# Layer 0's whole expert blocks in three products of rounded parts, with every third low part on GpSimd and a weight ring of ten

## The chip, the cores and the metric

The kernel runs on one core of a Trainium2 chip. A core has a matrix engine (TensorE, PE in the rows; PEld is its weight load), VectorE (DVE), ScalarE (ACT), GpSimd (POOL) and a queue that issues DMAs (SyncE, SP). The metric is the device time of one execution in microseconds, as the median of several runs. One execution is profiled; every row below is from that one.

## The reference, cut to what matters

Two layers. Each runs attention over 256 context and 256 latent tokens, then a mixture of experts. Layer 0 sends all 512 tokens through its experts, layer 1 only the 256 latent ones.

```
def swiglu(h, wg, wu, wd):
    return (jax.nn.silu(h @ wg) * (h @ wu)) @ wd

def moe(h, w_router, b_router, wg, wu, wd, sg, su, sd):
    ...                                  # gate: two of 16 experts for each token
    y = swiglu(h, sg, su, sd)            # the shared expert
    for e in range(N_EXPERTS):
        y = y + gate[..., e:e + 1] * swiglu(h, wg[e], wu[e], wd[e])
    return y
```

All arrays are float32. An expert's gate and up matrices are 1024 x 512, its down matrix is 512 x 1024: 2 MB each.

## The kernel before, in words

**Blocks and groups.** The chosen token slots of layer 0's experts are packed into 11 blocks of 128 rows. The most loaded of 14 experts has 128 slots, the next six have 96, the other seven 64, and two fixed experts have 128 each. So blocks 0, 9 and 10 hold one expert each ("whole" blocks), the others two, or parts of two with quarters of 32 rows. `GROUPS` orders them: [7, 8], [0, 6], [4, 5], [1, 2, 3], [9, 10]. A group runs all its gate products (`first`, then `silu`), all its up products (`first`, then `middle`), and its down products (`second`). Within a group each expert's matrix is loaded once (`matrix`, `got`). While a group's down products run, the next group's rows, gathered by indirect DMA (`bring`, `fetch`), are turned by TensorE (`turned`).

**Products.** Before, all expert blocks of layer 0 multiply plain float32 (`columns`): a block with several experts issues narrow products side by side, 64 or 32 columns wide, a whole block one of 128 columns. A plain float32 product shows in the trace as two instructions. Other matrices, the shared expert among them, are multiplied in rounded parts: `Stream.pieces` takes a loaded 128 x 2048 buffer in two pieces of 1024, ACT copies it to a high part of type float32r, DVE subtracts to get the low part, and `mm3` makes three products (high by high, high by low, low by high).

**Buffers.** Expert weights come through a ring of 1 MB buffers (`Stream.buf`): four of `rawp` and six of `raw2`, ten in all. The part buffers of the shared expert (`wpool`, three high and three low) are given back after group 2 (`w_es.close()`), and three more raw buffers take their place (`stE.further`, `RAW4`). `stE` is the stream of the loads, `stD` that of the part buffers. `shared_second`, the shared expert's down product, comes behind group 1.

**The end of the stage.** Blocks 0 to 8 scatter their results to DRAM (`scatter`). These are read back (`row_back`) in the last group into buffers of `raw2` and summed by `add_rows`: for each of four row tiles three operations on POOL for columns 0 to 511 and the same three on DVE for 512 to 1023. Blocks 9 and 10 keep their results on the chip as parts (`kept`). Behind a branch (`tc.If`, line 1643, for slots beyond the blocks) they are spread to the tokens' rows by products with a 0/1 matrix, `hits` (line 1687), which `own_rows` makes with eight comparisons. Layer 1 starts from there.

**Order.** A planner orders each engine's instructions when the program is built, from the program's order and a model of their times. On the chip each engine runs its own queue in order. Nothing is moved across the branch.

Of the kernel before, what the change touches and what calls it, by code (L numbers as in the profile page):

```python
# [11 lines left out]
F32 = mybir.dt.float32  # L12
F32R = mybir.dt.float32r
# [6 lines left out]
P = 128  # L20
D = 1024
KC = D // P
# [24 lines left out]
RAW4 = 3  # L47
# [12 lines left out]
SECOND_AT = 1  # L60
# [2 lines left out]
HIA = (5, 5)  # L63
RAW2 = 6
FPARTS = 3
EVERY = 5
GQ_AT = 10
STAT = 3
RAW3 = (4, 10)
# [69 lines left out]
def build(tc, I, out, dbg=None):  # L139
# [3 lines left out]
    def pool(st, name, bufs=1, **kw):  # L143
        if kw.get("space") is None:
            kw["reuse_waits"] = "tile"
        return st.enter_context(tc.tile_pool(name=name, bufs=bufs, **kw))
# [21 lines left out]
    def sc_bank(name="sc"):  # L168
        return pq.tile([P, 512], F32, tag="mm", name=name)

    def tr_bank(name="tr"):
        return pt.tile([P, 512], F32, tag="tr", name=name)

    def f(ap):
        return ap.bitcast(F32)
# [222 lines left out]
    def load_gq(l):  # L398
        nc.gpsimd.dma_start(out=gq, in_=I["gq"][l:l + 1].to_broadcast([P, 2 * QK + 2 * HD]))

    def layer(l):
# [341 lines left out]
        def evac(i, o, src):  # L743
            (nc.scalar.copy if i % 2 == 0 else nc.vector.tensor_copy)(out=o, in_=src)
# [461 lines left out]
        def shares(b):  # L1206

            qs_ = QUARTERS[l][4 * b:4 * b + 4]
            n = 4 if qs_[0] == qs_[3] else 2 if qs_[0] == qs_[1] and qs_[2] == qs_[3] else 1
            return [(32 * i, 32 * n, qs_[i]) for i in range(0, 4, n)]  # L1210

        def columns(o, x, ws, start, stop):

            for c0, n, w in ws:
                js_ = slice(c0, c0 + n)
                nc.tensor.matmul(o[js_], x[:, js_], w, start=start, stop=stop, tile_position=(0, c0))  # L1216
# [198 lines left out]
        else:  # L1415
# [50 lines left out]
            yprev = []  # L1466
            stE = Stream(tc, [rawp] + raw2)

            def shared_second():
                for blk in range(2):  # L1470
                    pbs = [mm_bank() for t in range(NT)]
                    for i, ws in enumerate(stD.pieces(stE.raw(I["w_s_down"][l, blk], 4, 512), 4, 512)):
                        for t in range(NT):
                            th, tl = (ep.tile([P, 2, P], F32R, tag="s" + c, name="s" + c, bufs=2) for c in "hl")
                            split(th, tl, sh[:, 2 * i:2 * i + 2, t * P:(t + 1) * P])
                            for k in range(2):
                                mm3(pbs[t], th[:, k], tl[:, k], *ws[k], i == 0 and k == 0, i == 1 and k == 1)
                    for t in range(NT):
                        add_result(t, blk, pbs[t], ep.tile([P, 512], F32, tag="hs", name="tm"))
# [9 lines left out]
            def evac(i, o, src):  # L1489
                return (nc.scalar.copy if i % 2 == 0 else nc.vector.tensor_copy)(out=o, in_=src)  # L1490

            eb = [3]

            def turned(x_):

                xt = ep.tile([P, KC, P], F32, tag="xt", name="xt", bufs=eb[0])
                for half_ in range(2):
                    tb = tr_bank()
                    for k in range(4):
                        kk = half_ * 4 + k  # L1500
                        nc.tensor.transpose(tb[:, k * P:(k + 1) * P], x_[:, kk * P:(kk + 1) * P], ident)
                    evac(half_, xt[:, half_ * 4:half_ * 4 + 4], tb.rearrange("p (k s) -> p k s", k=4))
                return xt

            def first(xt, ws):

                pb = sc_bank("pgu")
                for k in range(KC):
                    columns(pb, xt[:, k], [(c0, n, w[k // 4][:, k % 4]) for c0, n, w in ws], k == 0, k == KC - 1)
                return pb  # L1510

            def silu(pg):
                h_ = ep.tile([P, 512], F32, tag="hs", name="hs")
                ACT(h_, pg, AF.Silu)
                return h_

            def middle(h_, pu, gate_):

                tb = pm.tile([P, 512], F32, tag="md", name="ht")
                ht = ep.tile([P, 4, P], F32, tag="ht", name="ht", bufs=eb[0])  # L1520
                nc.vector.scalar_tensor_tensor(out=h_, in0=pu, scalar=gate_, in1=h_, op0=ALU.mult, op1=ALU.mult)  # L1521
                for k in range(4):
                    nc.tensor.transpose(tb[:, k * P:(k + 1) * P], h_[:, k * P:(k + 1) * P], ident)
                evac(1, ht, tb.rearrange("p (k s) -> p k s", k=4))
                return ht

            def second(ht, ws, yo, rest=None):
                for b in range(2):
                    pb = m2_bank()
                    for k in range(4):  # L1530
                        columns(pb, ht[:, k], [(c0, n, w[b][:, k]) for c0, n, w in ws], k == 0, k == 3)
                    x = slice(b * 512, (b + 1) * 512)
                    if rest is None:
                        evac(b, yo[:, x], pb)
                    else:
                        split(yo[:, x], rest[:, x], pb)
# [12 lines left out]
            def matrix(nm, got, b):  # L1549

                ws = []
                for c0, n, r in shares(b):
                    if r not in got:
                        got[r] = [stE.raw(s_, 4, 512) for s_ in halves(nm, by_rank(r))]
                    ws.append((c0, n, got[r]))
                return ws
# [8 lines left out]
            def own_rows():  # L1565

                h_ = ep.tile([P, 2 * NT, P], F32R, tag="xt", name="hits", bufs=eb[0])
                rowf = ep.tile([P, 2 * NT], F32, tag="rowf", name="rowf", bufs=1)
                for i, b in enumerate(own):
                    for t in range(NT):  # L1570
                        x = i * NT + t
                        TS(out=rowf[:, x:x + 1], in0=tab[:, b, 0:1], scalar1=float(-t * P), scalar2=None, op0=ALU.add)
                        TS(out=h_[:, x], in0=iota_r, scalar1=rowf[:, x:x + 1], scalar2=None, op0=ALU.is_equal)
                return h_
            X = [turned(x_) for x_ in bring(GROUPS[l][0])]
            for g_, g in enumerate(GROUPS[l]):
                nxt = GROUPS[l][g_ + 1] if g_ + 1 < len(GROUPS[l]) else []
                xg = bring(nxt)
                if g is own:
                    hits = own_rows()  # L1580
                got = {}
                hg = [silu(first(x_, matrix("w_e_gate", got, b))) for x_, b in zip(X, g)]
                got = {}
                H = [middle(h_, first(x_, matrix("w_e_up", got, b)), f(tab)[:, b, 1:2]) for h_, x_, b in zip(hg, X, g)]
                got = {}
                X = []
                for i, b in enumerate(g):
                    w = matrix("w_e_down", got, b)
                    if b == own[0]:
                        k_ = fp_.tile([P, 2, D], F32R, tag="sh", name="kept", bufs=1)  # L1590
                        kept[b] = k_[:, 0], k_[:, 1]
                    if b == own[1]:
                        kept[b] = yo_tile(F32R), yo_tile(F32R)
                    if b in own:
                        second(H[i], w, *kept[b])
                    else:
                        yo = yo_tile()
                        second(H[i], w, yo)
                        scatter(yo, tab[:, b, 2:3])
                    X += [turned(x_) for x_ in (xg[i:] if i + 1 == len(g) else xg[i:i + 1])]  # L1600
                if g_ == 0:
                    for s in strs:
                        get_row(gt2[:, s], l, 3, s)
                if g_ == SECOND_AT:
                    shared_second()
                if g_ == SECOND_AT + 1:
                    w_es.close()
                    stE.further(*[pool(x_pool, f"raw4{l}", RAW4)] * RAW4)
                if g_ == 2:
                    load_gq(l + 1)  # L1610
            mod_cols(l + 1)

            def add_rows(t, y0, y1):
# [64 lines left out]
            ep = ep_  # L1678


            for t in range(NT):
                for c in range(2):
                    pb = mm_bank("yl")
                    x = slice(512 * c, 512 * c + 512)
                    for i, b in enumerate(own):
                        for j in range(2):
                            nc.tensor.matmul(pb, hits[:, i * NT + t], kept[b][j][:, x], start=i + j == 0, stop=i + j == 2)
                    tm = ep.tile([P, 512], F32, tag="hs", name="tm")
                    add_result(t, c, pb, tm, (GT, TT)[c])
                if t < STAT:  # L1690
                    stat[t] = row_stat(t, tm)
# [92 lines left out]
```

## Time and profile before

| | |
|---|---|
| median of 3 runs | 1355.2 us (1353.67 to 1358.99) |
| profiled execution | 1353.72 us |
| its span, first to last instruction | 1351.9 us |
| mean granted TensorE clock | 0.978 |
| busy: PE / DVE / ACT / POOL | 92% / 47% / 30% / 29% |
| layer 0's expert blocks | about 509 to 812 us of the span |
| expert weights read there | 96 loads of 1 MB |

A row of a timeline gives start, duration, engine, source line, operation, tiles (out<-in) with their shape and how many were merged; in brackets the idle time before and what ended it. A row of a group gives the busy time and the mean duration of one. A granted clock of 1.00 is 2.4 GHz, 0.50 is 1.2 GHz.

### The profile page before, as it was taken

The numbers are of one execution on the slowest core, as the hardware profiler recorded it, in microseconds if no ns is written. First come the engines' busy times: TensorE is split into PE (matmuls) and PEld (weight loads), VectorE is DVE, ScalarE is ACT, GpSimd is POOL, SyncE is SP. The second block draws the span as 40 slices with busy tenths as digits, with TensorE's granted clock in tenths as the row PEclk, the third lists the DMA queues.
The fourth block names the chain that finished last, engine by engine and source line by source line (L and its number), as shares of the span: only waits on it lengthen the run. The fifth ranks groups of instructions, "written<-read, shape, count | busy, mean of one in ns | idle before, by whom it ended". The sixth has DMA issues, their size and how long they took to land. (4 is left out here: it accounts for less than half of the span.)

```text
span 1351.9 us, 19615 instructions
## 1 busy us (share of the span) xinstructions
PE 1248.2 (92%) x7338; PEld 787.1 (58%) x7338; DVE 632.2 (47%) x1503; ACT 400.4 (30%) x828; POOL 388.6 (29%) x473
## 2 busy tenths in 40 slices
PE   5998999899998989999999987899899989989986
PEld 2887886575786663345333346897566874446422
DVE  3547518886556440115102057685885652440212
ACT  3524226574322310002000016454554321110100
POOL 5038305673225010102100053382662200220211
PEclk8999999999999999999999998999999989999999
DMA  9332418504844479998899651335337869899995
GB/s 369 133 142 89 156 61 321 196 6 152 321 190 156 159 315 372 423 426 371 333 379 427 268 202 67 140 126 209 127 133 275 330 265 426 356 379 426 427 427 240
DMA packets 63129, 348.66 MB, mean 258 GB/s; under 512 B 7531, under 2 KB 15139, under 8 KB 26160
## 3 DMA queue, kind: packets, MB, share of 16 engines
q1 hardware_dynamic: 58256, 334.52, 62.2%
q0 software_dynamic: 4048, 10.66, 2.1%
q10 hardware_dynamic: 720, 2.12, 0.4%
q8 instruction: 61, 1.00, 0.3%
q14 instruction: 44, 0.36, 0.1%
HBM read 333.74 MB, written 16.29 MB: 259 GB/s over the span
## 5 line engine op out<-in xcount | busy, mean ns | idle before, releaser
L1216 PE MATMUL pgu<-raw,xt 128*32 128x512 f32 (+2 forms) x800 | 166.7, 601 | 0.5 <-DMA raw<-in_w_e_gate_dram 0.5
L120 DVE TENSOR_TENSOR lo<-raw,hi 128x1024 fp32r<-128x1024 f32 (+1 forms) x96 | 117.3, 1244 | 46.0 <-ACT hi L118 45.7
L1216 PEld LDWEIGHTS pgu<-raw,xt 128*32 128x32 f32 (+2 forms) x800 | 53.5, 131 | 103.3 <-issue 100.2
L118 ACT CAST hi<-raw 128x1024 fp32r<-128x1024 f32 (+1 forms) x96 | 96.0, 1034 | 41.6 <-PE mm L252 28.1
L805 POOL TENSOR_TENSOR pr<-pr,rs 128x512 f32<-128x512 f32 x80 | 82.9, 1044 | 59.7 <-DVE rs L804 30.7
L1216 PE MATMUL pgu<-raw,xs 128*64 128x512 f32 (+1 forms) x504 | 95.1, 596 | 2.1 <-DMA raw<-in_w_e_up_dram 1.8
L251 PE MATMUL mm<-hh,hi 128*128 128x512 f32 (+1 forms) x256 | 86.8, 342 | 3.0 <-ACT qb L591 2.7
L252 PE MATMUL mm<-hl,hi 128*128 128x512 f32 (+1 forms) x256 | 86.0, 339 | 0.0
L1216 PE MATMUL mm<-raw,ht 128*32 128x512 f32 (+2 forms) x400 | 84.1, 596 | 1.2 <-DVE yo L1490 0.8
L253 PE MATMUL mm<-hh,lo 128*128 128x512 f32 (+1 forms) x256 | 82.9, 338 | 0.5 <-DVE lo L120 0.5
L1228 POOL TENSOR_TENSOR xs<-xs,modsb 128x512 f32<-128x512 f32 x14 | 17.8, 1274 | 221.5 <-DVE modsb L1226 221.5
L251 PE MATMUL mm<-hi,hh 128*128 128x256 f32 (+2 forms) x176 | 60.3, 348 | 5.2 <-ACT hh L256 5.2
L1521 DVE SCALAR_TENSOR_TENSOR hs<-pgu,tab,hs 128x512 f32<-128x512 f32 x11 | 8.3, 751 | 121.4 <-PE pgu L1216 121.4
L253 PE MATMUL mm<-hi,hl 128*128 128x256 f32 (+2 forms) x176 | 59.7, 344 | 0.2
L252 PE MATMUL mm<-lo,hh 128*128 128x256 f32 (+2 forms) x176 | 59.5, 340 | 0.0
L1216 PEld LDWEIGHTS pgu<-raw,xs 128*64 128x64 f32 (+1 forms) x504 | 27.6, 123 | 53.6 <-issue 45.5
L799 DVE TENSOR_REDUCE mx<-sc 128x1 f32<-128x512 f32 (+1 forms) x80 | 54.2, 682 | 7.1 <-PE sc L759 4.6
L1216 PEld LDWEIGHTS mm<-raw,ht 128*32 128x32 f32 (+2 forms) x400 | 27.4, 130 | 48.4 <-issue 46.2
L251 PEld LDWEIGHTS mm<-hh,hi 128*128 128x128 f32 x256 | 49.2, 192 | 8.6 <-ACT qb L591 3.2
L1216 PE MATMUL mm<-raw,xs 128*64 128x512 f32 (+1 forms) x248 | 48.6, 597 | 4.3 <-DVE xs L1356 3.1
L252 PEld LDWEIGHTS mm<-hl,hi 128*128 128x128 f32 x256 | 49.2, 192 | 5.0
L326 PE MATMUL md<-raw,cs 128*32 128x256 f32 x640 | 45.2, 397 | 7.4 <-DMA raw<-in_w_mod_dram 7.4
(442 smaller groups left out, 2647.4 us busy)
## 6 DMA issues: line engine op xcount, KB each, us to landing
raw<-in_w_e_up_dram SPq DMA_DIRECT2D x64, 1024.0 KB, 16.1
raw<-in_w_e_gate_dram SPq DMA_DIRECT2D x63, 1024.0 KB, 13.6
raw<-in_w_e_down_dram SPq DMA_DIRECT2D x63, 1024.0 KB, 14.4
raw<-in_w_mod_dram SPq DMA_DIRECT2D x48, 1024.0 KB, 6.7
raw<-in_w_in_dram SPq DMA_DIRECT2D x20, 1024.0 KB, 5.0
raw<-in_w_out_dram SPq DMA_DIRECT2D x8, 1024.0 KB, 13.4
sgd<-gst SPq DMA_DIRECT2D x16, 256.0 KB, 2.0
yrows<-zero SPq DMA_DIRECT2D x4, 1024.0 KB, 12.1
```

The lines of the kernel that those rows point to most:

```text
L118: nc.scalar.copy(out=h, in_=v[:, k0:k0 + st])
L120: eng.tensor_tensor(out=lo, in0=v[:, k0:k0 + st], in1=h.bitcast(F32), op=ALU.subtract)
L251: nc.tensor.matmul(o, ah, bh, start=start, stop=False)
L252: nc.tensor.matmul(o, ah, bl, start=False, stop=False)
L253: nc.tensor.matmul(o, al, bh, start=False, stop=stop)
L326: nc.tensor.matmul(box[0][32 * j:32 * j + 32, :], cs32[:, l, k, :], w[:, kk, 256 * j:256 * j + 256], start=k == 0, stop=k == KC - 1, tile_ ...
L799: nc.vector.tensor_reduce(out=mx, in_=v, axis=AX.X, op=ALU.max)
L805: GT(out=pr, in0=pr, in1=rs.unsqueeze(2).to_broadcast([P, n, nkeys]), op=ALU.mult)
L1216: nc.tensor.matmul(o[js_], x[:, js_], w, start=start, stop=stop, tile_position=(0, c0))
L1228: add(out=xv, in0=xv, in1=tm, op=ALU.add)
L1521: nc.vector.scalar_tensor_tensor(out=h_, in0=pu, scalar=gate_, in1=h_, op0=ALU.mult, op1=ALU.mult)
```

## The change

The whole blocks 0, 9 and 10 go through `split_steps`: their turned rows and their middle results are split into high and low parts (`turned(..., True)`, `middle(..., True)`), their weights through `stD.pieces`, and each product becomes the three of `mm3`. The other eight blocks stay in plain float32. The part buffers are kept to the end of the groups, so the three further raw buffers are gone and the ring stays at ten. From the first group on every third low part of `stD` is subtracted on POOL instead of DVE (`EVERY`, now set for this stream). The tiles `xt` and `ht` get four buffers instead of three, the shared expert's split rows share those of `ht`, and `own_rows` moves from the start of the last group to behind the branch.

```
-EVERY = 5
+EVERY = 3
...
+            eb = [4]
...
+            def whole_block(b):
+                return len(shares(b)) == 1
+
+            def turned(x_, parts=False):
+
+                if parts:
+                    xt = [ep.tile([P, KC, P], F32R, tag="xt", name="xt" + c, bufs=eb[0]) for c in "hl"]
...
+                        split(*(a[:, half_ * 4:half_ * 4 + 4] for a in xt), tb.rearrange("p (k s) -> p k s", k=4))
+                    return xt
...
+                if isinstance(xt, list):
+                    split_steps(pb, xt, ws[0][2], KC)
+                    return pb
...
+            def split_steps(pb, xt, raws, n):
+                k = 0
+                for v in raws:
+                    for ws in stD.pieces(v, 4, 512):
+                        for wh, wl in ws:
+                            mm3(pb, xt[0][:, k], xt[1][:, k], wh, wl, k == 0, k == n - 1)
+                            k += 1
...
+                if parts:
+                    split(*ht, tb.rearrange("p (k s) -> p k s", k=4))
+                    return ht
...
+                    if isinstance(ht, list):
+                        split_steps(pb, ht, [ws[0][2][b]], 4)
...
-            X = [turned(x_) for x_ in bring(GROUPS[l][0])]
+            stD.every = EVERY
+            X = [turned(x_, whole_block(b)) for x_, b in zip(bring(GROUPS[l][0]), GROUPS[l][0])]
...
-                if g is own:
-                    hits = own_rows()
...
-                if g_ == SECOND_AT + 1:
-                    w_es.close()
-                    stE.further(*[pool(x_pool, f"raw4{l}", RAW4)] * RAW4)
...
+            w_es.close()
             mod_cols(l + 1)
...
+            eb[0] = 4
+            hits = own_rows()
             for t in range(NT):
```

## Rows read from the trace of the kernel before

**Rows 1.** The page's first part: busy time, share of the span, instructions.
```profile
PE 1248.2 (92%) x7338; PEld 787.1 (58%) x7338; DVE 632.2 (47%) x1503; ACT 400.4 (30%) x828; POOL 388.6 (29%) x473
```

**Rows 2.** Windows: engines' busy us (instructions), granted clock, DMA share, GB/s.
```profile
515.00:564.00 49.00, 48.23 (x221) 17.73 (x220) 6.34 (x9) 4.12 (x7) 5.99 (x6) 1.00 0.99 409
564.00:612.00 48.00, 47.12 (x169) 18.94 (x169) 5.46 (x8) 5.42 (x8) 4.06 (x4) 1.00 1.01 426
...
700.00:758.00 58.00, 58.00 (x414) 17.69 (x410) 8.76 (x22) 3.54 (x6) 1.95 (x2) 1.00 1.01 418
758.00:802.00 44.00, 42.71 (x108) 18.97 (x104) 13.16 (x16) 3.60 (x7) 17.20 (x13) 1.00 0.46 170
```

**Rows 3.** Groups of instructions by form, 470 to 850 us.
```profile
L1216 PE MATMUL pgu<-raw,xt 128*128 128x512 f32 x96 | 42.0, 595 | 0.0
...
L1216 PE MATMUL mm<-raw,ht 128*128 128x512 f32 x48 | 21.0, 594 | 0.0
...
L120 DVE TENSOR_TENSOR lo<-raw,hi 128x1024 fp32r<-128x1024 f32 x11 | 13.2, 1223 | 7.5 <-ACT hi L118 7.5
...
L118 ACT CAST hi<-raw 128x1024 fp32r<-128x1024 f32 x10 | 10.4, 1048 | 10.3 <-PE mm L252 5.0 <-issue 3.9 <-PE mm L253 1.1
```

**Rows 4.** Timeline of PE in groups 1 to 3.
```profile
604.91 7.09 PE L1216 MATMUL mm<-raw,ht 128*64 128x512 f32 x32 [0.39 <-issue]
...
614.26 0.40 PE L253 MATMUL mm<-hi,sl 128*128 128x512 f32 x1
614.49 0.40 PE L251 MATMUL mm<-hi,sh 128*128 128x512 f32 x1
...
686.96 34.48 PE L1216 MATMUL pgu<-raw,xt 128*32 128x512 f32 x238
```

**Rows 5.** Waits of PE, 500 to 640 us: total, times, longest.
```profile
PE pgu L1216 <- DMA raw<-in_w_e_gate_dram: 0.5, 1, 0.5
```

**Rows 6.** Timeline of SP: the issue of a load.
```profile
583.27 0.33 SPq L99 DMA_DIRECT2D raw<-in_w_e_down_dram  x1
```

**Rows 7.** The same issue and one at 642.72, us to landing.
```profile
raw<-in_w_e_down_dram SPq DMA_DIRECT2D x1, 1024.0 KB, 20.2
...
raw<-in_w_e_up_dram SPq DMA_DIRECT2D x1, 1024.0 KB, 4.8
```

**Rows 8.** POOL operations of two lines: ns min/median/max, first and last start.
```profile
L897 POOL TENSOR_TENSOR gates<-gates x8: 727/735/1723, 1045.8 to 1061.9; 128x256 f32<-128x256 f32 x8
...
L1617 POOL TENSOR_TENSOR raw<-raw x3: 1257/1262/1272, 781.4 to 791.9; 128x512 f32<-128x512 f32 x3
```

**Rows 9.** Timeline of POOL in the last group.
```profile
793.12 1.72 POOL L1619 TENSOR_TENSOR xs<-xs,y 128x512 f32<-128x512 f32 x1
794.80 1.72 POOL L1618 TENSOR_TENSOR raw<-raw,gt 128x512 f32<-128x512 f32 x1
```

**Rows 10.** Timeline of DVE, at 431 us and in the last group.
```profile
431.73 3.44 DVE L120 TENSOR_TENSOR lo<-raw,hi 128x1024 fp32r<-128x1024 f32 x2
...
793.75 1.64 DVE L1618 TENSOR_TENSOR raw<-raw,gt 128x512 f32<-128x512 f32 x1
...
796.99 0.68 DVE L257 TENSOR_TENSOR kept<-mm,kept 128x512 fp32r<-128x512 f32 x1
...
804.69 0.69 DVE L1619 TENSOR_TENSOR xs<-xs,raw 128x512 f32<-128x512 f32 x1
```

**Rows 11.** Timeline of POOL at 431 us.
```profile
431.95 2.13 POOL L991 TENSOR_TENSOR fr<-fr,B 128x512 f32<-128x512 f32 x1 [1.46 <-DVE fr L988]
```

**Rows 12.** Groups of DVE, 730 to 760 us.
```profile
L1573 DVE TENSOR_SCALAR hits<-iota_r,rowf 128x128 fp32r<-128x128 f32 x8 | 1.6, 277 | 0.0
```

**Rows 13.** Windows, PE alone: busy us, granted clock, DMA share, GB/s.
```profile
817.20:824.00 6.80, 3.87 (x15) 0.50 0.00 0
```

**Rows 14.** Timeline of PE in this stretch.
```profile
821.44 0.55 PE L252 MATMUL mm<-lo,hh 128*128 128x416 f32 x1
821.79 0.58 PE L253 MATMUL mm<-hi,hl 128*128 128x416 f32 x1
```

More of the change, by code (lines that the diff above doesn't have):

```diff
@@ L1473, in shared_second @@
                         for t in range(NT):
-                            th, tl = (ep.tile([P, 2, P], F32R, tag="s" + c, name="s" + c, bufs=2) for c in "hl")
+                            s_ = ep.tile([P, 2, 2, P], F32R, tag="ht", name="s", bufs=eb[0])
+                            th, tl = s_[:, 0], s_[:, 1]
                             split(th, tl, sh[:, 2 * i:2 * i + 2, t * P:(t + 1) * P])
@@ L1490, in evac @@
                 return (nc.scalar.copy if i % 2 == 0 else nc.vector.tensor_copy)(out=o, in_=src)
-            eb = [3]
-            def turned(x_):
+            def whole_block(b):
[3 more added lines that the diff above has]
+                    xt = [ep.tile([P, KC, P], F32R, tag="xt", name="xt" + c, bufs=eb[0]) for c in "hl"]
+                    for half_ in range(2):
+                        tb = tr_bank()
+                        for k in range(4):
+                            kk = half_ * 4 + k
+                            nc.tensor.transpose(tb[:, k * P:(k + 1) * P], x_[:, kk * P:(kk + 1) * P], ident)
+                        split(*(a[:, half_ * 4:half_ * 4 + 4] for a in xt), tb.rearrange("p (k s) -> p k s", k=4))
+                    return xt
                 xt = ep.tile([P, KC, P], F32, tag="xt", name="xt", bufs=eb[0])
@@ L1515, in silu, with middle @@
                 return h_
-            def middle(h_, pu, gate_):
+            def middle(h_, pu, gate_, parts=False):
                 tb = pm.tile([P, 512], F32, tag="md", name="ht")
-                ht = ep.tile([P, 4, P], F32, tag="ht", name="ht", bufs=eb[0])
+                ht = [ep.tile([P, 4, P], F32R if parts else F32, tag="ht", name="ht", bufs=eb[0]) for _ in range(1 + parts)]
                 nc.vector.scalar_tensor_tensor(out=h_, in0=pu, scalar=gate_, in1=h_, op0=ALU.mult, op1=ALU.mult)
@@ L1523, in middle @@
                     nc.tensor.transpose(tb[:, k * P:(k + 1) * P], h_[:, k * P:(k + 1) * P], ident)
-                evac(1, ht, tb.rearrange("p (k s) -> p k s", k=4))
-                return ht
+                if parts:
+                    split(*ht, tb.rearrange("p (k s) -> p k s", k=4))
+                    return ht
+                evac(1, ht[0], tb.rearrange("p (k s) -> p k s", k=4))
+                return ht[0]
             def second(ht, ws, yo, rest=None):
@@ L1529, in second @@
                     pb = m2_bank()
-                    for k in range(4):
-                        columns(pb, ht[:, k], [(c0, n, w[b][:, k]) for c0, n, w in ws], k == 0, k == 3)
+                    if isinstance(ht, list):
+                        split_steps(pb, ht, [ws[0][2][b]], 4)
+                    else:
+                        for k in range(4):
+                            columns(pb, ht[:, k], [(c0, n, w[b][:, k]) for c0, n, w in ws], k == 0, k == 3)
                     x = slice(b * 512, (b + 1) * 512)
@@ L1583, in layer @@
                 got = {}
-                H = [middle(h_, first(x_, matrix("w_e_up", got, b)), f(tab)[:, b, 1:2]) for h_, x_, b in zip(hg, X, g)]
+                H = [middle(h_, first(x_, matrix("w_e_up", got, b)), f(tab)[:, b, 1:2], whole_block(b)) for h_, x_, b in zip(hg, X, g)]
                 got = {}
@@ L1599, in layer @@
                         scatter(yo, tab[:, b, 2:3])
-                    X += [turned(x_) for x_ in (xg[i:] if i + 1 == len(g) else xg[i:i + 1])]
+                    X += [turned(xg[j], whole_block(nxt[j])) for j in range(i, len(nxt) if i + 1 == len(g) else min(i + 1, len(nxt)))]
                 if g_ == 0:
```

## The prediction

> **What bounds the kernel now.** I read first the page's totals: TensorE (PE) is busy 92% of a span of 1351.9 us, VectorE (DVE) 47%, ScalarE (ACT) 30%, GpSimd (POOL) 29% [rows 1]. That says only that PE is the first suspect. The change touches layer 0's experts alone, so I then cut that stage into stretches [rows 2]. From 515 to 758 PE hardly stops, but the DMA engines are as full: share 0.99 to 1.01 up to 612 and again after 700. In the last group, blocks 9 and 10 (758 to 802), PE is still full while the DMA share falls to 0.46: only there can faster products turn into time at once. In that same stretch POOL is busy 17.2 of 44 us and DVE 13.2; what they do there comes below.
>
> **What three products save.** A whole block's matmul is two instructions in plain fp32: its 72 products over the three whole blocks (8 gate, 8 up, 8 down each) are x96 + x48 instructions that hold PE 42.0 + 21.0 us, 875 ns a product and 21.0 us a block [rows 3]. A product of parts is three instructions; in the shared expert they start 0.23 us apart, so 0.69 us [rows 4]. The saving is 0.185 us x 72 = 13.3 us, 4.4 us a block: 4.4 in group 1 (block 0) and 8.9 in the last group.
>
> **What of it is kept in group 1.** Block 0 shares its group with block 6, and there PE runs at the pace of the loads. It waits 0.5 us for a gate load in this group [rows 5]; block 6's down product starts at 604.91 [rows 4], and its third load, issued at 583.27 [rows 6], lands 20.2 us later [rows 7], at 603.47. Block 0's 4.4 us end in a wait for that load, but for 604.91 - 603.47 = 1.4 us. I take 1.4, bounds 0 and 3 (a wait for the shared expert's parts may shrink too). PE was full from 700 to 758 [rows 2] and the last group began at 758.1, so it now starts at 756.7.
>
> **The ring of ten.** The three buffers that go were used only from the loads of group 3 on. With ten, a load there waits for the tenth load before it. Group 3's blocks hold PE 7 us per matrix (three blocks, gates and ups: the 34.48 us from 686.96 hold most of them [rows 4]), so buffers come free every 3.5 us. The first of group 3's fourth gate pair is free about 704.6, when block 3 has used it; the load that takes it is the first down weight, which PE wants after six such matrices, near 729. An unqueued load lands 4.8 us after issue [rows 7]. The same count leaves every later load 9 us or more before its use, so I cost it at nothing; if the cover were gone, the price would be a few waits of 1 to 3 us.
>
> **The conversions.** Each 1 MB load of a whole block becomes two pieces of two k-slices: ACT copies the high part (1.05 us), DVE subtracts for the low part (1.22 us) [rows 3], and every third piece is subtracted on POOL. PE uses up a piece in 6 x 0.23 = 1.38 us. Last group: 24 pieces, 16 on DVE, 8 on POOL (the counter stands at 24 when it begins). ACT has 25 us of copies in 33 us: enough. POOL has no 128x1024 operation before. Its 128x512 two-input ones take 1.26 us, its 128x256 ones 0.73 [rows 8], so 0.53 more per 256 and 2.33 us for 1024. Bounds: 1.27 (no dearer than 512) and 3.4 (twice the 1.72 of a disturbed one [rows 9]).
>
> **Where the saving goes.** In the same stretch POOL and DVE do the row sums of the scattered results: 12 operations each, POOL 1.27, DVE 0.69 alone. Started together they don't run side by side: POOL starts at 793.12 and 794.80 and takes 1.72, DVE from 793.75 takes 1.64 [rows 9, 10]. DVE's end at 795.39 is POOL's end (794.84) plus 0.55, so it waited for all of it, and POOL's second one for DVE's; from 793.12 to 794.80 a pair takes 1.68 us. The operation at 796.99, which reads PSUM, takes its 0.68 with POOL running. The subtraction in question does the same: two of them take 3.44 us against POOL's fr at 431.95 [rows 10, 11], the second ending 1.09 us after POOL let go. So the low parts on POOL and on DVE follow one another. The Trainium skill (SBUF — State Buffer, section Who interferes with whom) has this as an exclusive lock: a DVE instruction with two SBUF inputs and a GpSimd instruction that reads SBUF block each other for the whole instruction; by it, moving every third subtraction to POOL adds 8 x (2.33 - 1.09) = 10 us to the queue rather than taking any away, and the trace agrees with its 3.44 us for two.
>
> The sum for the last group: three pieces are ready when PE starts it (three part buffers). Of the other 21, 14 on DVE at 1.09 to 1.15 are 15.7 us and 7 on POOL 16.3; the row sums add 12 pairs of 1.68 = 20.2. Together 52.2 us, one after another, from the first freed part buffer plus its copy (1.38 + 1.05, say 2.5 us). 756.7 + 2.5 + 52.2 = 811.4. Before, DVE's last row sum ended at 804.69 + 0.69 = 805.4 [rows 10], and DVE takes the branch behind it. That is 6.0 us later, though PE's own work shrank by 8.9. For PE the pieces alone, with waits for the low part, end near 756.7 + 38 (each POOL piece is some 0.7 us late with three part buffers, 2.33 against 1.22); the row sums hold the end, or push PE if they come between.
>
> **The moved rows.** `own_rows` goes from group 4's start, where DVE was idle, to behind the branch; nothing covers it there. Its eight comparisons hold DVE 1.6 us [rows 12], and eight tiny ones beside them; the final products wait for them. I take 1.7 us, bounds 1 and 3. The extra splits when rows are turned and in `middle` read PSUM, cost ACT and DVE 0.6 to 0.7 us each, and lie under PE in groups 0 to 3 (DVE busy 8.76 of 58 us in group 3 [rows 2]): nothing. Four instead of three `xt` and `ht` buffers: nothing, no wait on them is in the trace [rows 5].
>
> Sum: +6.0 + 1.7 = +7.7 us. The profiled execution took 1353.72 (its span of 1351.9 plus 1.8), so it would take 1361.4; the runs' median lies 1.5 above it at 1355.2, so I forecast 1355.2 + 7.7, rounded to **1363 us**. Its own range is 1358 to 1370: POOL's last row sums may fall behind the branch (3 x 1.27 = 3.8 less, and group 1 may give 1 more), or POOL's subtraction lies at its upper bound (7 x 1.07 = 7.5 more).
>
> **The rivals.** *The parts keep up and the end comes earlier.* If the row sums and POOL's subtractions fit beside DVE's, PE decides: 24 x 1.38 = 33.2 us plus 1 of transposes from 756.7, so PE ends at 790.9 instead of 801.8 (its last stretch ends at 802 [rows 2]), 10.9 earlier. With the 1.7 of the moved rows that is 1355.2 - 9.2 = 1346; with the 38 us of late POOL pieces, 1351. For it: the subtractions and row sums are 57 us of work on two engines that have 34 us each. Against it: [rows 9 to 11]. It begins to win where the chain of 52.2 us falls under 44.5 (756.7 + 2.5 + 44.5 + 1.7 is the old 805.4), that is, where more than 7.7 us of POOL's 16.3 run beside DVE. *A draw.* If POOL's 1024 takes 1.27 rather than 2.33 us, 7 x 1.06 = 7.4 us go and the result is 1355.5; about the same comes out if half of the row sums slip under the work after the branch. *PE's clock falls.* After pauses PE was granted 0.50 from 817.2 to 824 with 3.87 of 6.8 us busy [rows 13], the lower level (1.2 GHz), where products of 416 columns started 0.35 us apart [rows 14], so 0.43 for 512. A last group all at that level needs 24 x 6 x 0.43 = 62 us plus 1 from 756.7, PE's end at 819.7, 14.3 us behind DVE's old 805.4: with the moved rows 1355.2 + 14.3 + 1.7 = 1371. Against it: the low stretch shown is 6.8 us long, and the whole group would have to run so. The Trainium skill (TensorE: Matmul & The Clock Gate, section A second HAM failure mode) tells of a kernel whose frequent short pauses between groups of matmuls made the clock oscillate; no run here shows that yet. *The ring is short.* Waits of 1 to 3 us in groups 3 and 4: on top of the forecast, 1366.
>
> **Chances.** Forecast 0.50, parts keep up 0.16, draw 0.19, clock 0.09, ring 0.06. One measurement of this kernel tells about 0.5% (6.8 us) from no change: faster means under 1348.4, slower over 1362.0. Faster takes three quarters of the second case: 0.12. Slower takes two thirds of the forecast's range (1362 to 1370 of 1358 to 1370), the clock and the ring: 0.48. The rest, 0.40, is the same. The range 1348 to 1372 leaves out half of the fast case and what lies beyond the clock's: under 0.2. Cases of both signs are in it; the forecast's own range stands above.
>
> **What would show it.** Right: products of parts 0.69 us each at full clock in blocks 0, 9, 10; POOL subtractions of 128x1024 near 2.3 us or above, DVE's between 1.2 and 3.5; PE waiting for `lo` in the last group; the branch after layer 0 left near 811; the comparisons of `own_rows` behind it. Group 2 begins one to two us earlier, not four. Wrong if DVE's and POOL's subtractions overlap without stretching, if POOL does 1024 in the time of 512, if the row sums start late and are hidden behind the branch, or if a load is what PE waits for in groups 3 and 4.

## The result, and the profile after

The changed kernel takes 1388.0 us (median of 6 runs, 1382.1 to 1391.3) against 1355.2 (6 runs, 1353.7 to 1360.1): a ratio of 1.0226, 95% interval 1.0205 to 1.0246. The forecast was 1363, its range 1348 to 1372. The sign was right, the size was 33 us in place of 8. The profiled execution of the changed kernel took 1391.3 us (span 1389.6), the slowest of its six.

The page's totals answer to [rows 1]: PE is busy 13.5 us more, though 72 fp32 products became cheaper (its granted clock is lower on the mean, 0.957 against 0.978).

```profile
PE 1261.7 (91%) x7410; PEld 814.0 (59%) x7410; DVE 680.5 (49%) x1528; ACT 439.2 (32%) x870; POOL 428.3 (31%) x487
```

The stretches of the changed kernel, cut at its own milestones (columns as in [rows 2]): group 1; the shared expert with groups 2 and 3; the last group; from its last product to layer 1's first transposes.

```profile
569.60:624.20 54.60, 47.50 (x203) 23.70 (x201) 18.07 (x22) 16.73 (x24) 13.40 (x8) 1.00 1.01 426
624.20:771.70 147.50, 145.21 (x904) 54.87 (x904) 33.95 (x47) 18.53 (x32) 23.41 (x16) 0.99 0.85 337
771.70:827.20 55.50, 43.22 (x156) 30.96 (x152) 42.71 (x37) 25.52 (x29) 33.89 (x17) 0.85 0.47 188
827.20:848.60 21.40, 9.99 (x32) 7.71 (x33) 17.79 (x25) 4.88 (x13) 12.60 (x9) 0.73 0.37 130
```

The same two last stretches of the kernel before:

```profile
758.10:801.80 43.70, 42.61 (x108) 18.97 (x104) 12.96 (x16) 3.43 (x6) 17.20 (x13) 1.00 0.46 170
801.80:816.60 14.80, 7.90 (x32) 5.88 (x33) 13.36 (x24) 4.93 (x13) 6.08 (x5) 1.00 0.49 189
```

The last group grew from 43.7 to 55.5 us: PE, idle for 1.1 before, is idle for 12.3. DVE went from 13.0 busy us to 42.7, POOL from 17.2 to 33.9, neither full over the whole of it. The granted clock, 1.00 before, is 0.85 there and 0.73 behind.

What PE waited for, 760 to 840 us (total, times, longest):

```profile
PE yl L1716 <- DVEq L1670: 8.2, 1, 8.2
PE mm L252 <- DVE lo L120: 4.5, 3, 3.5
PE pgu L252 <- POOL lo L120: 2.6, 3, 1.6
PE mm L251 <- DVE kept L257: 2.1, 1, 2.1
PE pgu L251 <- ACT hi L118: 1.6, 1, 1.6
PE mm L251 <- ACT hi L118: 1.4, 1, 1.4
```

The first wait is the branch behind DVE's last row sum; all others are for parts or for `kept`, none for a load.

The groups by form, 765 to 840 us, beside [rows 3]:

```profile
L120 DVE TENSOR_TENSOR lo<-raw,hi 128x1024 fp32r<-128x1024 f32 x16 | 28.1, 1788 | 13.7 <-ACT hi L118 13.7
L118 ACT CAST hi<-raw 128x1024 fp32r<-128x1024 f32 x21 | 21.6, 1049 | 19.5 <-PE pgu L253 14.6 <-PE mm L253 2.8 <-issue 2.0
L120 POOL TENSOR_TENSOR lo<-raw,hi 128x1024 fp32r<-128x1024 f32 x8 | 19.6, 2453 | 16.2 <-ACT hi L118 16.2
```

Read the last column as a ring: DVE and POOL wait for ACT's copy, ACT waits for PE to be done with a part buffer, and PE (waits above) waits for DVE and POOL. That is the group's first part. The windows up to the last gap of DVE and from there to its last row sum (columns as in [rows 2]):

```profile
779.41:804.97 25.56, 20.09 (x76) 14.99 (x77) 17.52 (x20) 13.22 (x14) 10.33 (x5) 0.93 0.61 240
804.97:834.69 29.72, 15.61 (x47) 10.27 (x45) 29.69 (x21) 7.76 (x10) 27.38 (x15) 0.70 0.30 103
```

In the first no engine is full, and each waits for the next. In the second DVE has no pause at all: pieces and row sums follow one another on it and on POOL.

Timelines of POOL and of DVE in that group (start, duration; in brackets the idle time before it) answer to [rows 9, 10]:

```profile
778.34 2.39 POOL L120 TENSOR_TENSOR lo<-raw,hi 128x1024 fp32r<-128x1024 f32 x1
783.43 2.39 POOL L120 TENSOR_TENSOR lo<-raw,hi 128x1024 fp32r<-128x1024 f32 x1 [2.71 <-ACT hi L118]
788.53 2.40 POOL L120 TENSOR_TENSOR lo<-raw,hi 128x1024 fp32r<-128x1024 f32 x1 [2.70 <-ACT hi L118]
...
805.47 2.28 POOL L1644 TENSOR_TENSOR raw<-raw 128x512 f32<-128x512 f32 x1
```

```profile
779.41 3.54 DVE L120 TENSOR_TENSOR lo<-raw,hi 128x1024 fp32r<-128x1024 f32 x2 [1.95 <-ACT hi L118]
784.74 3.31 DVE L120 TENSOR_TENSOR lo<-raw,hi 128x1024 fp32r<-128x1024 f32 x2 [1.78 <-ACT hi L118]
789.83 3.31 DVE L120 TENSOR_TENSOR lo<-raw,hi 128x1024 fp32r<-128x1024 f32 x2 [1.78 <-ACT hi L118]
793.06 0.86 DVE L1603 TENSOR_SCALAR hits<-iota_r,rowf 128x128 fp32r<-128x128 f32 x4
...
834.00 0.69 DVE L1646 TENSOR_TENSOR xs<-xs,raw 128x512 f32<-128x512 f32 x1
```

Three pieces take 5.10 us (783.43 to 788.53). DVE's pair starts at 784.74 and ends at 788.05, 2.23 after POOL's 785.82: DVE stood still until POOL was done, then did both. PE would need 3 x 1.38 = 4.14. The first row sum (on POOL) starts at 805.47, the last (on DVE) ends at 834.69.

### The profile page after: what moved, and what is told of

It is laid out like the page before. It is cut to its first block, busy times and chain, and to the rows that moved or that the text cites. A ratio compares the mean times of both kernels' runs of the same rounds, so it can differ in the third digit from the quotient of the medians.

```text
span 1389.6 us, 19870 instructions
## 1 busy us (share of the span) xinstructions
PE 1261.7 (91%) x7410; PEld 814.0 (59%) x7410; DVE 680.5 (49%) x1528; ACT 439.2 (32%) x870; POOL 428.3 (31%) x487
## 5 line engine op out<-in xcount | busy, mean ns | idle before, releaser
L120 DVE TENSOR_TENSOR lo<-raw,hi 128x1024 fp32r<-128x1024 f32 (+1 forms) x118 | 155.7, 1344 | 79.3 <-ACT hi L118 78.9
L118 ACT CAST hi<-raw 128x1024 fp32r<-128x1024 f32 (+1 forms) x132 | 132.5, 1038 | 67.0 <-PE mm L252 28.8
L1216 PE MATMUL pgu<-raw,xt 128*32 128x512 f32 (+1 forms) x704 | 126.5, 602 | 1.0 <-DMA raw<-in_w_e_gate_dram 1.0
L1216 PEld LDWEIGHTS pgu<-raw,xt 128*32 128x32 f32 (+1 forms) x704 | 35.9, 123 | 81.5 <-issue 79.5
L1216 PE MATMUL mm<-raw,ht 128*32 128x512 f32 (+1 forms) x352 | 63.3, 596 | 1.6 <-DVE yo L1493 1.6
L1569 POOL DMA_INDIRECT yrows<-yo,tab x9 | 10.2, 1133 | 138.2 <-DVE modA L372 56.0
L818 PE MATMUL ptr<-ident,pr 128*128 128x128 f32 x320 | 51.9, 287 | 0.4 <-DVE pt L744 0.2
## 6 DMA issues: line engine op xcount, KB each, us to landing
raw<-in_w_e_up_dram SPq DMA_DIRECT2D x64, 1024.0 KB, 12.3
raw<-in_w_e_down_dram SPq DMA_DIRECT2D x63, 1024.0 KB, 12.2
yrows<-zero SPq DMA_DIRECT2D x4, 1024.0 KB, 12.3
```

The lines of the kernel that those rows point to most:

```text
L118: nc.scalar.copy(out=h, in_=v[:, k0:k0 + st])
L120: eng.tensor_tensor(out=lo, in0=v[:, k0:k0 + st], in1=h.bitcast(F32), op=ALU.subtract)
L818: nc.tensor.transpose(tb[:, x:x + P], prs[j][:, i, c * P:(c + 1) * P], ident)
```

## The experiments

All kernels below but e4 are cut from the changed kernel. Stretches are from the profiled execution of each: A to B is from the experts' first product to the shared expert's first second product, B to C from there to the end of the last `mm` product of the last group, C to D to layer 1's first transposes (L458), D to end is layer 1. G to C is the part of B to C that belongs to the last group, from its first product on. The median and the ratio are of the timed runs, "before" taken on the same chip; the ratio is an estimate from all fast runs and not the quotient of two medians.

```
                          median  ratio (95% interval)      A-B    B-C   (G-C)   C-D  D-end
before                    1355.2                           102.7  189.9  (43.7)  14.8  535.3
after                     1388.0  1.0226 (1.0205-1.0246)   108.8  203.0  (55.5)  21.4  541.0
e1  no POOL third         1366.3  1.0101 (1.0076-1.0126)   108.7  193.7  (50.0)  15.4  536.9
e2  blocks 9, 10 only     1379.8  1.0191 (1.0173-1.0210)   103.7  203.0  (55.5)  21.5  538.7
e3  block 0 only          1363.8  1.0079 (1.0058-1.0101)   108.3  191.8  (41.9)  13.1  538.3
e4  before, ring of ten   1359.3  1.0025 (1.0006-1.0043)   102.5  189.8  (43.7)  14.4  538.4
e5  four part buffers     1376.2  1.0146 (1.0121-1.0171)   107.8  200.0  (49.9)  18.9  538.6
e6  e5, no POOL           1369.4  1.0098 (1.0079-1.0118)   110.0  193.1  (46.4)  18.8  538.9
e7  no row sums           1371.3  1.0129 (1.0107-1.0152)   107.9  193.5  (46.0)  16.5  540.7
e8  block 9 only, no POOL 1356.7  1.0010 (0.9997-1.0024)   104.2  184.8  (40.7)  19.3  537.0
e9  e7, no POOL           1357.4  1.0001 (0.9984-1.0019)   108.4  183.9  (40.1)  15.1  536.9
e10 e7, four buffers      1364.0  1.0066 (1.0045-1.0087)   106.8  193.2  (43.2)  16.2  536.0
e11 e1, order 6, 0        1365.5  1.0071 (1.0054-1.0088)   106.1  195.3  (49.8)  12.6  538.3
e12 0 and 9, order 6, 0   1358.5  1.0011 (0.9990-1.0032)   106.6  185.8  (40.3)  16.2  537.8
e13 fourth product        1391.2  1.0246 (1.0226-1.0266)   112.9  204.9  (56.3)  21.1  540.3
e14 e13, no POOL          1378.5  1.0154 (1.0132-1.0176)   111.0  202.6  (58.8)  14.3  537.3
e15 e10, no POOL          1359.6  1.0014 (0.9995-1.0032)   108.3  187.3  (40.6)  12.6  540.7
```

### One part of the change at a time: e1 to e4

```diff
 e1
-            stD.every = EVERY
+            stD.every = 0
 e2
-                return len(shares(b)) == 1
+                return len(shares(b)) == 1 and b != 0
 e3
+                return b == 0
 e4 (the kernel before)
                 if g_ == SECOND_AT + 1:
                     w_es.close()
-                    stE.further(*[pool(x_pool, f"raw4{l}", RAW4)] * RAW4)
```

> The changed kernel with every low part on VectorE again (EVERY 0 for that stream); all else as changed. Theory A (the low parts on GpSimd and VectorE and the row sums exclude one another): the chain of the last group loses 7 x 2.3 and gains 7 x 1.1, 8 us less, and PE's waits for POOL low parts go: about 1376. Theory B (the part buffers and the in-order queues of ScalarE and VectorE make PE wait, whoever subtracts): little moves, 1384 or more. Theory C (the ring of ten is what costs): 1388.

> Block 0 goes back to plain float32, blocks 9 and 10 stay in parts. The profile of the changed kernel has 6.0 us more in group 1, so by theories A and B alike 1388 - 6 = 1382, with group 1 as long as before (48.0 us). If group 1's loss were a late load (theory C), it would stay: 1388.

> Only block 0 is in parts, blocks 9 and 10 in plain float32; ring of ten and the moved rows stay. The last group up to layer 1 gave 11.8 + 4.0 + 2.6 = 18.4 us of the loss; without it 1388 - 18 = 1370, or 1364 if the 5.9 us that the profiled run lost before the experts is chance. Theory C: the last group stays late, 1380 or more.

> The kernel before without the three further buffers: a ring of ten throughout, nothing else. Theory C (the ring): 1365 to 1385. Theories A and B: no change, 1355 within 3 us, as the prediction worked out.

Every third subtraction on POOL costs 1388.0 - 1366.3 = 21.7 us by the medians, 17 by the ratios, and 15.4 between A and D of the profiled executions (333.2 against 317.8). These executions differ by 27.0 us; the rest of that lies ahead of A and in layer 1, where the two kernels have the same instructions. Each of the three prices is more than the 12 that theory A had for it. Without POOL's third, three products are still 1% slower than plain fp32. A to B grows by 6 us where block 0 is in parts (102.7 to 108.3 or more), with POOL or without; with block 0 plain the stretch is 103.7, so about 5 of the 6 are block 0's. The other 1 us is order: in all kernels cut from the changed one, 60 transposes (`tr`) run on PE between A and B, before only 52, and eight take 1.0 to 1.2 us. The ring of ten costs 0.25%, 3.4 us (0.8 to 5.8 by the interval), but the stretches of layer 0 show none of it (102.5, 189.8, 14.4): where it arises isn't settled.

In e1 the row sums alone stand where POOL's subtractions stood. DVE's and POOL's timelines of e1:

```profile
783.80 8.35 DVE L120 TENSOR_TENSOR lo<-raw,hi 128x1024 fp32r<-128x1024 f32 x4
```

```profile
784.37 2.25 POOL L1644 TENSOR_TENSOR raw<-raw 128x512 f32<-128x512 f32 x1
```

Four subtractions take 2.09 us each, and a row sum of 1.27 [rows 8] takes 2.2: they wait for one another, as [rows 9 to 11] had it.

### What the pieces cost, and what the row sums: e7, e9

```diff
 e7
-            for t in range(NT):
-                add_rows(t, *ys[t])
             x_pool.close()
 e9: the same with
+            stD.every = 0
```

> Changed kernel without the row sums of the last group: the 24 operations that add the scattered results of the other blocks are left out (the rows are still read back). The prediction's step had the row sums and the pieces as one chain of 52.2 us on DVE and POOL. If that chain is right, 20.2 us go: 1368. If in the changed kernel the pieces alone hold PE and the row sums only come at their end (805.5 to 834.7 in the profile), the end of PE at 827 moves little and only DVE's lateness of 7 us behind PE goes: 1381. Rival C (PE's low clock is what stretches the last group): no change of PE's end, 1381 too, and the low stretches stay.

> Changed kernel with all subtractions on DVE and without the row sums (24 operations that add the scattered results are left out). The last group then has nothing beside DVE's 24 subtractions. If the conversions by themselves can feed PE, the last group takes 24 x 1.38 + 4 = 37 to 39 us, against 46.0 in e7 (POOL at work, no row sums), 50.0 in e1 (row sums, POOL off) and 43.7 before: total 1355 to 1358. Rival C (PE's low clock after short pauses is the cause): 44 us or more, total 1362 or above.

B to C is 183.9 us with neither, 193.7 with the row sums, 193.5 with POOL's third, 203.0 with both. Each costs PE 10 us, and the two add up. The row sums' part lies in the last group (50.0 with them, 40.1 with neither). Of POOL's, 5.9 lie there (46.0 against 40.1) and 3.7 between B and G: that stretch is 143.8 us in e1 and e9, 147.5 in e7 and the changed kernel, where POOL also takes two pieces of the shared expert's down weights (at 625 and 636 us). In time, leaving out the row sums gives 16.7 us by the medians and 15.3 between A and D, under the 20.2 of the chain; PE's end moves by 9.5 and the stretch behind it, where the branch no longer waits for DVE, gives 5.0. So the theories that left PE's end in place fall. With neither, B to C falls 6.0 under the kernel before, but the last group only 3.5 (40.1 against 43.7), of the 8.9 reckoned. Block 0 takes it back ahead of B (A to B 108.4): from A to C e9 needs 292.3 us, the kernel before 292.6, so that e9 stands where the kernel before stands. The rival C (the last group at 44 us or more) falls with its 40.1. DVE's timeline in e9, with nothing beside it:

```profile
772.88 3.50 DVE L120 TENSOR_TENSOR lo<-raw,hi 128x1024 fp32r<-128x1024 f32 x3 [0.82 <-ACT hi L118]
776.72 1.22 DVE L120 TENSOR_TENSOR lo<-raw,hi 128x1024 fp32r<-128x1024 f32 x1 [0.34 <-ACT hi L118]
778.83 3.50 DVE L120 TENSOR_TENSOR lo<-raw,hi 128x1024 fp32r<-128x1024 f32 x3 [0.89 <-ACT hi L118]
```

Subtractions at 1.17 us again, four in 5.95 us: 1.49 a piece, a little over PE's 1.38.

### Exclusion or the round of a buffer: e5, e6, e10, e15

POOL's pieces are 2.4 us long, DVE's two come after them: 4.6 us of the 5.10. But with three buffers and every third piece on POOL, POOL always meets the same buffer, whose round is a copy (1.05), POOL (2.40), PE (1.38) and the hand-overs: about 5.1 as well. A fourth buffer tells them apart.

```diff
 e5
-RAW2 = 6
-FPARTS = 3
+RAW2 = 5
+FPARTS = 4
 e6: the same with
+            stD.every = 0
 e10: e5 without the row sums; e15: e6 without the row sums
```

> Changed kernel (POOL subtracts every third piece) with four part buffers in place of three; the eight kilobytes come from the ring, which has nine buffers. Theory A (exclusion: DVE's and POOL's subtractions follow one another, so three pieces cost 3.3 on DVE plus what POOL adds whatever the buffers): the last group's cycle of three pieces stays at 5 us and the stretch from the shared expert to layer 1 stays within 3 us of the 224.4 of the changed kernel. Theory B (the buffer loop: with three buffers and every third piece on POOL, POOL always meets the same buffer, whose round is copy 1.05 + POOL 2.4 + PE 1.38 + hand-overs = 5.1 us): a fourth buffer lets the cycle fall to 4.2 to 4.8 us, and the stretch to 215 or below; total near 1377.

> The same four part buffers and ring of nine, all subtractions on DVE. Beside e1 (three buffers, ring of ten, no POOL: 1366.3) it prices a buffer against a ring place: A and B both expect 1362 to 1368, stretch from the shared expert to layer 1 of 205 to 210. What the two theories differ in is the distance to e5: A 15 to 22 us, B 8 to 12 us.

> Changed kernel with four part buffers and a ring of nine, POOL subtracting every third piece, without the row sums (left out). Buffer loop alone (B): the fourth buffer gives POOL's piece four pieces' time (5.5 us) for its 5.1 us round, so the last group takes 38 to 40 us, as e9. Exclusion alone (A): two pieces on DVE and one on POOL take 4.8 us one after another, so 24 pieces take 38.4 us plus 4 = 42 to 44 us. Three buffers (e7) took 46.0.

> Four part buffers, ring of nine, all subtractions on DVE, row sums left out: the control for e10 (the same with POOL's third: 1364.0, 193.2 us from the shared expert to the last product) as e9 is for e7. If DVE and POOL exclude one another whatever the buffers (A), POOL's price stays near that of three buffers (9.6 us in that stretch): 183 to 185 us, 1354 to 1358. If the buffer loop is what costs (B), e10 has lost it already: 190 to 193 us, 1361 to 1364.

Neither theory has it alone: e5 meets B's time and A's cycle, e6 lies 6.8 us below e5, under what either had, e10's last group (43.2) is what A had, and e15's 187.3 lies between the two. With the row sums left out, POOL's third costs the last group 46.0 - 40.1 = 5.9 us with three buffers and 43.2 - 40.6 = 2.6 with four: more than half of it goes with the round, the rest stays. Between B and G it costs 3.7 and 3.3, and there the four runs with a ring of nine are 2.5 to 3 us longer than their pairs with ten; whether the ring or the fourth buffer does that, no run tells apart. In time, with the row sums, POOL's price falls from 21.7 to 1376.2 - 1369.4 = 6.8 us (between A and D from 15.4 to 4.9). Yet POOL's pieces in e5 still come 5.03 us apart on average, in the two intervals that there are:

```profile
776.32 2.40 POOL L120 TENSOR_TENSOR lo<-raw,hi 128x1024 fp32r<-128x1024 f32 x1 [1.70 <-ACT hi L118]
780.55 2.65 POOL L120 TENSOR_TENSOR lo<-raw,hi 128x1024 fp32r<-128x1024 f32 x1 [1.82 <-issue]
786.38 2.43 POOL L120 TENSOR_TENSOR lo<-raw,hi 128x1024 fp32r<-128x1024 f32 x1 [3.18 <-PE pgu L253]
```

### PE's clock: e13, e14

PE's low clock was a rival. Between B and D the changed kernel's profile has 32 us at 0.50, the kernel before none. A fourth product, low by low, fills PE's waits:

```diff
 e13 (split_steps)
-                            mm3(pb, xt[0][:, k], xt[1][:, k], wh, wl, k == 0, k == n - 1)
+                            mm3(pb, xt[0][:, k], xt[1][:, k], wh, wl, k == 0, False)
+                            nc.tensor.matmul(pb, xt[1][:, k], wl, start=False, stop=k == n - 1)
 e14: the same with
+            stD.every = 0
```

> Changed kernel with a fourth product (low part by low part) at each k-slice of blocks 0, 9 and 10: 72 more instructions of 0.23 us, 16.9 us more work for PE, 5.6 of it in group 1, in the places where PE now waits for parts. Theory W (only the late parts cost time, PE's clock is a bystander): where PE waited it now works, the end is set by the conversions as before or a little later: 1388 to 1398. Theory K (the short waits let PE's clock fall, 20.5 us at 0.50 between the shared expert and the last product and 11.5 behind it, and that costs some 10 of the 33 us): with the waits filled the granted clock stays at 1.00 in the last group, low time there falls below 8 us, and the total comes out below 1385 in spite of the added work.

> The same fourth product with all subtractions on DVE (e1: 1366.3, 13.7 us at the low clock between the shared expert and the last product). W: 1368 to 1378. K: 1362 to 1367, low time there under 5 us.

Both come out slower, not faster, so K's times are missed. But 16.9 us of added work cost e13 only 3.2 us over the changed kernel (1391.2), and of the 11 us that were added between B and C only 1.9 show there: most of it went into waits, though some may be hidden by the low clock, which fell from 20.5 to 10.2 us there. Without POOL the same work costs 12.2 (1378.5 against 1366.3). The waits were filled only in part (20.4 us at 0.50 between B and D are left), so these two runs don't price the low clock; the trace of the changed kernel bounds it (below). POOL's timeline of e13 shows the round once more:

```profile
785.51 2.40 POOL L120 TENSOR_TENSOR lo<-raw,hi 128x1024 fp32r<-128x1024 f32 x1 [3.02 <-ACT hi L118]
791.11 2.41 POOL L120 TENSOR_TENSOR lo<-raw,hi 128x1024 fp32r<-128x1024 f32 x1 [3.20 <-ACT hi L118]
```

5.60 us apart in place of 5.10: a piece of PE's is two products longer (0.46), and the round has grown by that.

### Group 1: e11; a version to beat both: e8, e12

In group 1 of the changed kernel ACT and PE show (timelines):

```profile
585.81 0.60 ACT L1538 ACTIVATE hs<-pgu 128x512 f32<-128x512 f32 x1 [7.48 <-PE pgu L1216]
586.30 2.93 ACT L118 CAST hi<-raw 128x1024 fp32r<-128x1024 f32 x3
```

```profile
587.39 0.49 PE L251 MATMUL pgu<-hi,xth 128*128 128x512 f32 x1 [1.62 <-ACT hi L118]
588.65 0.50 PE L252 MATMUL pgu<-lo,xth 128*128 128x512 f32 x1 [0.77 <-DVE lo L120]
```

The copies for block 0's up weights stand on ACT behind the silu of block 6, which waits for PE's last gate product (up to 585.8); only then do they begin, and PE waits.

```diff
 e11 (e1 and)
-GROUPS = (([7, 8], [0, 6], [4, 5], ...
+GROUPS = (([7, 8], [6, 0], [4, 5], ...
 e8 (e1 and)
-                return len(shares(b)) == 1
+                return b == 9
 e12 (e11 and)
+                return b in (0, 9)
```

> e1 (all subtractions on DVE) with the order of group 1 changed from 0, 6 to 6, 0: the plain block goes ahead of the block in parts. Theory Q (in e1 block 0's high-part copies stand on ACT behind the silu of block 6, and its low parts on DVE behind block 6's products, so PE waits): the 6 us of group 1 go, because PE has a plain matrix of 7 us before each matrix in parts: first product of the experts to the shared expert's first 102 to 105 us (108.7 in e1, 102.7 before), total 1360 to 1363. Theory L (loads pace the group whatever the order): 107 to 109 us, 1366.

> Changed kernel with only block 9 in three products, blocks 0 and 10 plain, all subtractions on DVE. The plain block's matrices (7 us of PE each) then give the twelve pieces twice the time. Theory A: block 9's 4.4 us are saved in full, the ring costs 3: 1352 to 1355. Rival: the row sums on POOL still stand in the way of DVE's twelve pieces and PE waits for a few of them: 1357 to 1360.

> All subtractions on DVE, blocks 0 and 9 in parts, block 10 plain, group 1 in the order 6, 0. If Q holds, block 0 costs nothing and may give 1 to 2 us: 1354 to 1357, beside 1356.7 of block 9 alone. If L holds: 1361 to 1363.

With the plain block first, A to B is 106.1, 2.6 us less than in e1, as Q had it in part, and its waits for copies are gone. But B to G grows from 143.8 to 145.6, so that at the last group's start only 0.8 us is left of it (251.7 from A, in e1 252.5). What PE still waits for in e11, 511 to 617 us, is loads and one low part:

```profile
PE pgu L1216 <- DMA raw<-in_w_e_gate_dram: 2.3, 1, 2.3
PE mm L252 <- DVE lo L120: 1.5, 1, 1.5
...
PE pgu L1216 <- DMA raw<-in_w_e_up_dram: 0.7, 1, 0.7
```

Q and L are each right for a part, and the total hardly moved (1365.5). e8 ends PE's work 5.1 us earlier than the kernel before by B to C (184.8), 3.7 by A to C, and loses 4.5 again behind it (C to D 19.3 against 14.8); its 1356.7 is above what A had, at the lower edge of its rival. The window from its last product to layer 1:

```profile
799.10:818.40 19.30, 10.98 (x33) 8.05 (x33) 16.09 (x28) 4.93 (x13) 5.98 (x6) 0.73 0.38 144
```

Its DVE ends the row sums 191.7 us behind B, where the kernel before has 193.5, so the branch came only 1.8 earlier (0.3 from A), and the granted clock of this window was 0.73. e12, with block 0 in parts behind block 6, is no better (1358.5, above what Q had, under what L had). Neither e8 nor e12 can be told from the kernel before; none beats it.

## Why the prediction was wrong in size

The profiled executions, 1389.6 and 1351.9 us, differ by 37.7; by milestones of the two:

- **Ahead of the experts: +6.2** (515.4 against 509.2), forecast 0. PE's and POOL's instructions are the same there. Over all these kernels the experts' start lies between 505.7 and 515.4, so this is the run's and not the change's.
- **Groups 0 and 1: +6.0**, forecast -1.4. This step failed. The saving was bounded by the loads alone ("bounds 0 and 3"); that parts for one block come through queues which another block's silu and products hold was not priced. About 1 us of the 6 is eight transposes that moved ahead of B. e11 takes 2.6 away and gives 1.8 of it back behind B; the rest is loads, late low parts and switching (last section), not priced one by one.
- **The shared expert to the last group's start: +1.4**, forecast 0. Two terms hide in it. With all subtractions on DVE (e1) the stretch is 2.4 shorter than before; POOL's two pieces of the shared expert's weights add 3.8, for one of which PE waits 2.3. The prediction priced POOL's subtractions in the last group alone and put the others at nothing.
- **The last group, from its start to DVE's last row sum: +15.7** (47.3 to 63.0), forecast +7.4 (54.7). This is the step that failed in the main. The terms held: POOL's subtraction took 2.36 to 2.40 with one exception of 2.79 (forecast 2.33), the pair behind it 2.23 (forecast 2.2 to 2.3), and DVE and POOL did follow one another. (That POOL had no 128x1024 operation before was misread, it has three memsets of 0.95 us at line 1453; the sum does not use it.) By the Trainium skill (SBUF — State Buffer, Who interferes with whom) a DVE instruction with two SBUF inputs and a GpSimd one that reads SBUF block each other fully, and the 2.09 of e1 against 1.17 of e9 agrees. What was wrong was the sum: "52.2 us, one after another" takes a queue that never runs dry and an engine that does nothing else. From 774.50, where DVE subtracts again, to 834.69 are 60.2 us. In 53.3 of them a subtraction or a row sum is on DVE, or POOL is at work, near the 52.2. In 3.4 DVE does other work by itself (comparisons, `hs`, splits), which the sum left out, and in 3.5 both stand still; nearly all of these 6.9 lie before 804.97. DVE alone stands still for 10.0 us up to then, in seven gaps (three of them are in the rows above), but in 6.5 of them POOL works, which the sum counts already. The chain came out 8.3 longer than summed. The ring from PE's freed buffer through ACT to DVE and POOL has no slack with three buffers (e13; the fourth buffer takes 2.8 us off the last group in e10 against e7), and the prediction counted work and not rounds: "the pieces alone end near 756.7 + 38" was 46.0 us in e7.
- **From there to layer 1: +2.7**, forecast 1.7, but for another reason. `own_rows` stands behind the branch in the program, but its comparisons ran at 793.06 and 794.51, ahead of the branch, so the move cost nothing behind it; that nothing is moved across the branch does not hold for them. The final products ran at the low clock for a while (0.50 from 830.4 to 840.5): rows of two products start 0.86 us apart, later ones 0.46 (timeline of PE, changed kernel).

```profile
836.42 1.05 PE L1716 MATMUL yl<-yo,hits 128*128 128x512 f32 x2
837.28 1.05 PE L1716 MATMUL yl<-kept,hits 128*128 128x512 f32 x2
...
842.95 0.62 PE L1716 MATMUL yl<-yo,hits 128*128 128x512 f32 x2
843.41 0.63 PE L1716 MATMUL yl<-kept,hits 128*128 128x512 f32 x2
```

- **Layer 1: +5.7**, forecast 0. The fifteen experiments lie between 536.0 and 540.7 here, all above the 535.3 of the kernel before. The instructions are the same in both, and the granted clock is 0.96 against 0.97. How much of it belongs to the change stays open, as does the place of the ring's 3 us.

Right were the price of a product of parts (0.23 us apart in the last group too, three a product), the wait for `lo` in the last group, no wait for a load in groups 3 and 4, the exclusion, and the work that it puts one after another. Of the rivals, with both blocks in parts they kept up in no run: even with no row sums and no POOL (e9) a piece took 1.49 us. The low clock came (32 us of it), on top of the forecast's chain and not in its place. It adds little to that chain: in the last group the clock is at 0.50 from 799.6 to 803.0, where nine products start 0.43 us apart in place of 0.23 and so hold up DVE by at most 1.8 us, and again from 813.3 to 826.9, where DVE, for which the branch waits, has no gap left. Behind the last row sum it costs at most some 2 us, by the rows above.

## What to carry to other kernels

When work moves from one engine to a chain of three, don't sum each engine's work: follow one buffer round its ring (copy, subtract, product, free), count the buffers, and compare round over buffers with what the consumer needs for a piece (here 5.10 / 3 = 1.70 us against 1.38). Add what else stands in the queues of the engines, which was harmless as long as they had time to spare. Putting every n-th piece on a slow engine with n buffers sends it always to the same buffer, and if that engine excludes the other one, it takes work from nobody. And before cheapening PE's products, look at what ends just behind PE: here the row sums on DVE and POOL ended 3.6 us behind PE's last product (805.4 against 801.8), so they needed the time that the change gave away.

## What the runs showed of the hardware

Not only two-input instructions are held up. In e13 seven comparisons, each with one 128x128 tensor (0.2 us apart when alone: four take 0.86 above), took 3.61 us. Six of them started before POOL's subtraction; the seventh started 0.13 after it, took 2.43 in place of 0.28, and ended 0.08 after POOL let go. In e1 two took 1.15 and 1.29 beside row sums of POOL.

```profile
795.89 3.61 DVE L1604 TENSOR_SCALAR hits<-iota_r,rowf 128x128 fp32r<-128x128 f32 x7
```

```profile
796.94 2.48 POOL L120 TENSOR_TENSOR lo<-raw,hi 128x1024 fp32r<-128x1024 f32 x1 [3.42 <-ACT hi L118]
```

The Trainium skill (SBUF — State Buffer, Who interferes with whom) says that a `tensor_scalar` too can contend with GpSimd, in a mode that uses both ports; the 2.43 agrees, if such a mode was in use, which the trace doesn't say.

Where the two kinds of product are mixed on PE, time is lost at the change. One plain product (two instructions) among products of parts, in group 1 of the changed kernel:

```profile
574.93 0.40 PE L251 MATMUL pgu<-hi,xth 128*128 128x512 f32 x1
575.26 1.07 PE L1216 MATMUL pgu<-raw,xt 128*64 128x512 f32 x2
576.26 0.50 PE L252 MATMUL pgu<-lo,xth 128*128 128x512 f32 x1
576.60 0.40 PE L253 MATMUL pgu<-hi,xtl 128*128 128x512 f32 x1
```

From 574.93 to 576.60 are 1.67 us for four instructions; at the 0.23 of products of parts and the 0.24 of these halves in a row (30 in 7.08 us) it would be 0.94. Three such places in group 1 (at 575.26, 591.64 and 612.42) take 2 us of the saving. What in the change takes the time, the trace doesn't say.
